# Sums of the first layer's gate and up weights moved into the first projection, and the context's gate and up products in scaled half-precision pairs

## The chip, the cores and the metric

The kernel runs on one core of one Trainium2 chip. The core has a matrix engine (PE, with its weight loads shown apart as PEld), a vector engine (DVE), a scalar engine (ACT), a general engine (POOL, also called GpSimd), and a queue engine (SP) that only issues transfers. Each of them takes its instructions in the order of its own program, and semaphores tie them together. The metric is the time of one execution in device microseconds (us); less is better. Three executions of the kernel before gave 2910.8, 2915.75 and 2916.38 us, a median of 2915.75 us.

## The reference: what is computed

The model has two layers on 1024 latent tokens and 256 context tokens of width 1024, all in float32. Cut to what matters:

```python
def swiglu(u, w_gate, w_up, w_down):
    return (jax.nn.silu(u @ w_gate) * (u @ w_up)) @ w_down

for i in range(DEPTH):                       # two layers
    ...                                      # adaLN, then a mixer, as below
    y_lat, y_ctx = mixer(...)                # layer 0: Fourier and Hyena; layer 1: neighbourhood attention
    h_lat = h_lat + g1 * y_lat
    h_lat = h_lat + g2 * swiglu(modulate(rms_norm(h_lat, norm2_g[i]), sh2, sc2), ffn_w_gate[i], ffn_w_up[i], ffn_w_down[i])
    if not last:                             # only layer 0 has a context FFN
        h_ctx = h_ctx + cg1 * y_ctx
        h_ctx = h_ctx + cg2 * swiglu(modulate(rms_norm(h_ctx, norm2_g[i]), csh2, csc2), ffn_w_gate[i], ffn_w_up[i], ffn_w_down[i])
return rms_norm(h_lat, final_g)
```

The hidden width is 2816, which the kernel cuts into 22 blocks of 128. Latent and context tokens share all weights.

## The kernel before

**Precision.** PE multiplies at full rate only in reduced formats, so every product is taken as three: an operand is split into a high part and the rest, and high·high, high·low and low·high are summed. Two kinds of pairs are in use. In the float32 kind (`split`, L285 to L289) the two parts are rounded float32 tiles ("fp32r" in the profile; the matmuls then show as f32). In the half-precision kind (`half_split`, L1215 to L1219) ACT multiplies the source by a scale and rounds it to f16 (L1218), and DVE computes the rest in one operation (L1219). The half kind needs a scale for each weight, which keeps it in the range of f16. It is found from the sums of the absolute values: `abs_sums` (L1247) has ACT read a 128x1024 tile and add up (L1251), writing the values themselves into a scratch tile `junk` of the pool T; `scale_cols` (L1311) then adds over partitions with one small matmul and takes a bound and its reciprocal on DVE (L1316 to L1318).

**Stages.** In the order of time: filters of the Hyena part; the first projection (`in_proj`, about 205 to 460 us of the profile), in half pairs, 16 blocks of 72 matmuls; Hyena and Fourier transforms; the output projection (`out_proj`, about 724 to 846 us), first for context tokens and the first 512 latent ones, then for the other 512; the context's gate and up products (851 to 983 us); the latent gate and up products of layer 0 by a Strassen-Winograd scheme with 11 pairs of blocks (983 us on); the down product; then layer 1 with attention.

**The context's gate and up products** stand at the head of `ffn` (L1519 on). For each of the 22 blocks the gate and the up weight (512 KB each) are loaded by SP into a tile of the pool S4 (20 tiles), split into float32 pairs by ACT and DVE, and multiplied with the context activations `uf`: 24 matmuls of 128x256 each. ACT applies Silu (L1529), DVE multiplies (L1530), POOL stores the result. The pair tiles come in turn from three sets of two tiles, the tags "wh"/"wl" twice and "ws" once (`pair3`), in the last two blocks from "wh"/"wl" alone (`pair1`). Between the blocks, one step of `wino_second` prepares Winograd operands of the latent activations.

**The Winograd products** (`wino_weights`, L1395 on) load four quarters of a weight, one half of them into a "ws" tile (two exist) and the other into S4. Where a weight's scale isn't known (`if key not in self.wsc`), they are summed on the spot: two passes on ACT and the chain behind. In layer 0 it is known for block pair 0 alone; for pairs 1 to 10 it is summed there.

**Sums taken ahead.** `qkv_sums` (L1253) runs beside `out_proj`, three 512 KB loads after each of its 16 output blocks: 44 loads into S4 tiles, issued by POOL, each followed by one `abs_sums` pass on ACT. The first four are gate and up of layer 0, pair 0; then come the attention's weights, then gate and up of layer 1, pairs 0 and 1.

**What sets the order.** The program text isn't the order of the engines: a planner in the framework walks through the instructions with its own estimate of their durations and gives each engine a fixed order, the earlier text first among what is ready. Work without inputs, such as a load, can so come far ahead of its place. On the chip the order stays as planned: an instruction that waits holds all behind it on its engine. Tiles of a pool are reused, so a load can also wait for the last reader of the tile.

**Beside the first projection** run `fill` generators: `filt` (the context's filters, one step per output block; their constants are loaded into "ws" tiles) and `ada` (32 reductions of adaLN weights, loaded by SP, two per block; DVE line L470, half of which write into tiles of T). T has 6 tiles and, in this stage, 4 more of the pool TK.

**After the first half of `out_proj`** (`after1`), the context activations are normalised: DVE and ACT write `uf` in float32 pairs (`norm_block`), unscaled.

Of the kernel before, what the change touches and what calls it, by code (L numbers as in the profile page):

```python
# [19 lines left out]
P = 128  # L20
# [11 lines left out]
KSTART = (0, 8, 24, 32)  # L32
PAD_C, PAD_T, SHIFT = 176, 160, 16
BOPS = ("B11", "B21", "T2", "T1", "T3", "B22", "T4")
# [167 lines left out]
class Builder:  # L202
# [176 lines left out]
    def weights16(self, src, scale, w=1024, cut=False, load=None):  # L379
        st = self.pw.tile([P, 1024], F32, tag="ws", name=self.nm("ws"))  # L380
        hi, lo = (self.pw.tile([P, 1024], F16, tag=g, name=self.nm(g)) for g in ("wh", "wl"))
        (load or self.ld)(st.rearrange("p (n k) -> p n k", n=4) if cut else st[:, :w], src)
        self.half_split(st[:, :w], scale, hi[:, :w], lo[:, :w])
        return hi, lo

# [829 lines left out]
    def half_split(self, src, scale, hi, lo):  # L1215

        nc = self.nc
        nc.scalar.activation(hi, src, AF.Copy, scale=scale)  # L1218
        nc.vector.scalar_tensor_tensor(lo, src, scale, hi, op0=MUL, op1=SUB)  # L1219

# [32 lines left out]
    def qkv_sums(self):  # L1253

        a = self.a
        self.qs = self.C(44)
        src = [a["wv"][ch, kp] for ch in range(2) for kp in range(4)]
        src += [a[n][b] for n in ("wq", "wk", "w_out2") for b in range(KB)]
        for l, i in ((0, 0), (1, 0), (1, 1)):
            src += [a[n][l, 2 * i + k] for n in ("gate", "up") for k in (0, 1)]  # L1260
        for j, k in enumerate((32, 33, 34, 35, *range(32), *range(36, 44))):
            t = self.S4()
            self.ldr(t, src[k])
            self.abs_sums([t], self.qs[:, k:k + 1])
            if j % 3 == 2:
                yield
        yield

    def first_scales(self, l):

        keys = [(l, i, m) for i in range(l + 1) for m in (0, 1)]
        n, k = len(keys), 3 * len(self.wsc)
        q = self.qs[:, 32 + 4 * l:36 + 8 * l]
        s, inv = self.scale_cols(q, self.wcol, k, n)
        for j, key in enumerate(keys):
            self.wsc[key] = (s[:, j:j + 1], inv[:, j:j + 1])
# [214 lines left out]
    def ffn(self, l, u, h, hs, second, after, keep=None, begun={}):  # L1491
# [28 lines left out]
        if u is not None:  # L1520
            for fb in range(NFB):
                wide = 3 if fb < NFB - 2 else 2
                gh, gl = self.weights(a["gate"][l, fb], wide=wide)
                uh, ul = self.weights(a["up"][l, fb], wide=wide)
                lo = self.last_lo
                ga = self.lin(gh, gl, 0, range(KB), u, (2,))[2]
                ua = self.lin(uh, ul, 0, range(KB), u, (2,))[2]
                t = self.T()
                nc.scalar.activation(t[:, :256], ga[:, :256], AF.Silu)  # L1529
                nc.vector.tensor_tensor(t[:, :256], ua[:, :256], t[:, :256], MUL)  # L1530
                self.ldr(hidc[fb // 2][:, fb % 2], t[:, :256])
# [590 lines left out]
    def run(self):  # L2122
# [98 lines left out]
        for i in range(8):  # L2221
            self.tap(f"u{i}", u.ap(0, i, 0))
        self.in_proj(u, ((filt, 1), (ada, 2)))
        drain(ada)
# [58 lines left out]
        def after1(pcs):  # L2283
            spill(h, hs0, pcs)
            if 0 in pcs:
                uf.t.update(self.new_act(pcs=(2,)).t)
                rs = self.rms(pcs)
                for b in range(KB):
                    self.norm_block({b: h.ap(0, b, 2)}, b, 2, 0, 3, uf, rs[0])
                load_h((1,))  # L2290
                self.ucol, self.usi = self.operand_scale(0, 3, (0, 1))
                self.first_scales(0)
                for _ in self.wino_first(h, 0, 3, rs[1]):
                    pass
            else:
                rest.append(self.rms((1,))[0])
# [215 lines left out]
```

## Time and profile before

| what | value |
|---|---|
| median of three executions | 2915.75 us (2910.8 to 2916.38) |
| the profiled execution's own time | 2919.95 us |
| its span from first to last instruction | 2918.2 us |
| mean granted PE clock | 0.977 |
| read from and written to memory | 455.33 MB and 135.53 MB |

The profile is of one execution, which took 4.2 us more than the median. In its rows, a matmul's duration is longer than the distance to the next, since matmuls are pipelined: the pace is read from the starts. "[2.33 <-ACT wh L287]" behind a row says that the engine was idle for 2.33 us before it and that ACT's line 287, writing the tile wh, ended that. "x2" means two instructions in a row. In a table of windows each engine's column is its busy time in us with the count of its instructions, followed by the granted PE clock, the share of time that the transfer engines were busy, and GB/s.

### The profile page before, as it was taken

The page shows a single profiled execution, that of the slowest core. Times are in us where ns is not written, and L with a number is a line of the kernel's source. Part 1 is how long each engine was busy: PE and PEld are TensorE (multiplying, and loading weights), DVE is VectorE, ACT ScalarE, POOL GpSimd, SP SyncE. Part 2 cuts the span into 40 slices and gives each one's busy share as a digit, 9 for nine tenths or more (in the row PEclk, how much of TensorE's full clock was granted, in tenths as well). Part 3 has the DMA queues.
Part 4 walks back from the last instruction along what each step waited for, and adds up shares of the span by engine and source line. Part 5 has one row for each costly group of instructions (what it writes and reads, how often), then busy time and mean ns, then how long its engine had stood idle before and what let it go on. Part 6 is the DMA issues. An engine that isn't in the chain of part 4 may idle for free. (4 is left out here: it accounts for less than half of the span.)

```text
span 2918.2 us, 46050 instructions
## 1 busy us (share of the span) xinstructions
PE 2766.6 (95%) x16163; PEld 1714.2 (59%) x16163; DVE 2094.0 (72%) x3833; ACT 1647.7 (56%) x2899; POOL 642.6 (22%) x1057
## 2 busy tenths in 40 slices
PE   6989999999989999999999999999999999999998
PEld 3766557888879644444555844676665444444554
DVE  4778867585467798877886767776676778775765
ACT  4674324454675667654555555676664477654553
POOL 1012013354220121213120012444443022112000
PEclk8989999999999999999999999999999999999999
DMA  6574434358785555566994798777775666424753
GB/s 254 187 265 161 161 122 151 111 168 286 285 344 182 207 205 197 201 213 240 327 333 161 273 337 294 179 188 172 185 198 188 236 226 231 153 93 184 242 191 113
DMA packets 325156, 615.98 MB, mean 211 GB/s; under 512 B 90934, under 2 KB 130552, under 8 KB 324922
## 3 DMA queue, kind: packets, MB, share of 16 engines
q1 hardware_dynamic: 252378, 384.38, 39.9%
q0 software_dynamic: 70240, 224.45, 21.6%
q10 hardware_dynamic: 2304, 4.20, 0.4%
q8 instruction: 127, 2.08, 0.3%
q14 instruction: 107, 0.88, 0.1%
HBM read 455.33 MB, written 135.53 MB: 202 GB/s over the span
## 5 line engine op out<-in xcount | busy, mean ns | idle before, releaser
L1449 PE MATMUL ps<-s,s 128*128 128x512 f16 x2592 | 582.2, 382 | 14.4 <-ACT tk L1454 6.8
L1449 PEld LDWEIGHTS <-s 128*128 128x128 f16 x2640 | 259.0, 98 | 332.6 <-issue 27.8
L283 PE MATMUL ps<-s,wh 128*128 128x256 f32 (+3 forms) x1752 | 398.2, 331 | 11.1 <-ACT wh L287 5.4
L1218 ACT ACTIVATE s<-s,c 128x512 f16<-128x512 f32 (+1 forms) x324 | 233.5, 754 | 141.9 <-DMA s<-d 79.9
L1219 DVE SCALAR_TENSOR_TENSOR s<-s,c,s 128x512 f16<-128x512 f32 (+1 forms) x324 | 247.4, 794 | 84.5 <-ACT s L1218 84.1
L1666 PE MATMUL ps<-s 128*128 128x512 f16 (+2 forms) x1308 | 303.4, 378 | 2.0 <-DVE s L1219 2.0
L283 PE MATMUL pq<-s,wh 128*128 128x512 f16 (+1 forms) x1000 | 280.3, 354 | 9.8 <-DMA wh<-d 5.4
L283 PE MATMUL ps<-s,wl 128*128 128x256 f32 (+3 forms) x876 | 261.6, 331 | 1.3 <-DVE wl L289 1.2
L283 PEld LDWEIGHTS <-wh 128*128 128x128 f16 x1664 | 160.9, 99 | 170.2 <-issue 20.9
L1666 PEld LDWEIGHTS <-s 128*128 128x128 f16 x1536 | 148.5, 98 | 178.9 <-issue 6.5
L274 POOL DMA_DIRECT2D d<-s x201 | 109.0, 543 | 640.5 <-DVE s L1510 178.6
L283 PE MATMUL ps<-s,s 128*128 128x65 f16 (+5 forms) x2666 | 222.3, 236 | 27.5 <-DMA s<-s 11.4
L335 ACT CAST mat<-cs 128x1024 fp32r<-128x1024 f16 (+2 forms) x120 | 111.6, 935 | 140.6 <-PE ps L283 57.3
L283 PEld LDWEIGHTS ps<-s,wh 128*128 128x128 f32 x1088 | 177.5, 192 | 18.1 <-ACT wh L287 5.7
L283 PE MATMUL ps<-s,mat 128*128 128x512 f32 x696 | 184.7, 413 | 3.3 <-DVE s L289 2.9
L1449 PE MATMUL ps<-s,wh 128*128 128x512 f16 x616 | 184.9, 379 | 1.8 <-DVE g L1463 1.4
L283 PE MATMUL pq<-s,wl 128*128 128x512 f16 (+1 forms) x500 | 174.5, 354 | 0.5 <-DMA wl<-d 0.5
L283 PEld LDWEIGHTS <-s 128*128 128x128 f16 x2400 | 114.5, 98 | 82.9 <-DMA s<-s 11.5
L283 PEld LDWEIGHTS ps<-s,mat 128*128 128x128 f32 x696 | 136.5, 199 | 37.9 <-DVE s L289 3.8
L1251 ACT ACTIVATE t<-s 128x1024 bf16<-128x1024 f32 (+1 forms) x164 | 141.9, 867 | 12.2 <-DVE c L470 8.4
L283 PEld LDWEIGHTS ps<-s,s 128*128 128x128 f32 (+1 forms) x746 | 113.6, 192 | 32.1 <-ACT s L287 7.0
L283 PEld LDWEIGHTS <-wl 128*128 128x128 f16 x832 | 82.3, 99 | 77.4 <-issue 4.5
(431 smaller groups left out, 5477.3 us busy)
## 6 DMA issues: line engine op xcount, KB each, us to landing
s<-d SPq DMA_DIRECT2D x294, 256.0 KB, 4.0
d<-s POOLq DMA_DIRECT2D x157, 256.0 KB, 3.2
s<-in_down SPq DMA_DIRECT2D x154, 256.0 KB, 5.4
s<-in_ada_w POOLq DMA_DIRECT2D x48, 512.0 KB, 4.8
g<-in_bias POOLq DMA_DIRECT2D x128, 192.0 KB, 3.6
s<-in_gate SPq DMA_DIRECT2D x46, 512.0 KB, 3.7
s<-in_up SPq DMA_DIRECT2D x46, 512.0 KB, 4.0
d<-g POOLq DMA_DIRECT2D x87, 256.0 KB, 2.9
```

The source lines that it names most:

```text
L274: self.last_ldr = self.nc.gpsimd.dma_start(out, in_).ins
L283: self.nc.tensor.matmul(o, l, r, start=st, stop=sp)
L335: self.nc.scalar.copy(m, st)
L1218: nc.scalar.activation(hi, src, AF.Copy, scale=scale)
L1219: nc.vector.scalar_tensor_tensor(lo, src, scale, hi, op0=MUL, op1=SUB)
L1251: self.nc.scalar.activation(junk[:, :t.shape[1]], t, AF.Abs, scale=2.0 ** -15, accum_out=st[:, k:k + 1])
L1449: nc.tensor.matmul(ps, x[:, sl], y, start=first and j == 0 and x is wh and y is xh, stop=j == 3 and x is wl, skip_group_check=True)
L1666: m = nc.tensor.matmul(acc[j][:, c0:c1], x[:, sl], y[:, xs], start=first and k == 0, stop=last and k == 2, skip_group_check=True)
```

## The change

1. `qkv_sums` loses its first four loads; 40 remain, and the column block `qs` shrinks from 44 to 40.
2. A new generator `gate_sums` loads the gate and up weights of all 11 block pairs of layer 0 (44 loads of 512 KB, issued by POOL, into the two "ws" tiles) and sums each on ACT. It runs beside `in_proj` as a third `fill`, three loads per output block, and is drained behind it.
3. `first_scales(0)` takes scales for all 22 weights of layer 0 from these sums, so that `wino_weights` finds each key known and does no summing in layer 0.
4. The context's gate and up products use half pairs: `weights3` splits by `half_split` with the known scale, in the same three tile sets, and in all 22 blocks. The inverse scales go into the Silu (an argument of the ACT instruction) and into the product (a `scalar_tensor_tensor` with the inverse in place of `tensor_tensor`).
5. `uf` becomes scaled half pairs: `norm_half` in place of `norm_block`, behind `load_h((1,))` and `operand_scale`. It takes four tiles of the pool S2 where it took eight.
6. A padding tile shrinks from 176 to 136 columns to make room for 44 columns of sums.

```diff
-PAD_C, PAD_T, SHIFT = 176, 160, 16
+PAD_C, PAD_T, SHIFT = 136, 160, 16
...
+    def weights3(self, src, scale):
+        self.p3 = (getattr(self, "p3", 0) + 1) % 3
+        tags = ("ws", "ws") if self.p3 == 0 else ("wh", "wl")
+        st = self.S4()
+        hi, lo = (self.pw.tile([P, 1024], F16, tag=g, name=self.nm(n)) for g, n in zip(tags, ("wh", "wl")))
+        self.ld(st, src)
+        self.half_split(st, scale, hi, lo)
+        return hi, lo
...
     def qkv_sums(self):
-        self.qs = self.C(44)
+        self.qs = self.C(40)
         src = [a["wv"][ch, kp] for ch in range(2) for kp in range(4)]
         src += [a[n][b] for n in ("wq", "wk", "w_out2") for b in range(KB)]
-        for l, i in ((0, 0), (1, 0), (1, 1)):
-            src += [a[n][l, 2 * i + k] for n in ("gate", "up") for k in (0, 1)]
-        for j, k in enumerate((32, 33, 34, 35, *range(32), *range(36, 44))):
+        src += [a[n][1, 2 * i + k] for i in (0, 1) for n in ("gate", "up") for k in (0, 1)]
+        for j, k in enumerate(range(40)):
             t = self.S4()
             self.ldr(t, src[k])
             self.abs_sums([t], self.qs[:, k:k + 1])
...
+    def gate_sums(self):
+        a = self.a
+        self.fs = self.C(4 * (NFB // 2))
+        for j in range(4 * (NFB // 2)):
+            t = self.pw.tile([P, 1024], F32, tag="ws", name=self.nm("ws"))
+            self.ldr(t, a[("gate", "up")[j // 2 % 2]][0, j // 4 * 2 + j % 2])
+            self.abs_sums([t], self.fs[:, j:j + 1])
+            yield
...
     def first_scales(self, l):
-        keys = [(l, i, m) for i in range(l + 1) for m in (0, 1)]
+        keys = [(l, i, m) for i in range(2 if l else NFB // 2) for m in (0, 1)]
         n, k = len(keys), 3 * len(self.wsc)
-        q = self.qs[:, 32 + 4 * l:36 + 8 * l]
+        q = self.qs[:, 32:40] if l else self.fs
...
             for fb in range(NFB):
-                wide = 3 if fb < NFB - 2 else 2
-                gh, gl = self.weights(a["gate"][l, fb], wide=wide)
-                uh, ul = self.weights(a["up"][l, fb], wide=wide)
+                (gs, gi), (us, ui) = (self.wsc[(l, fb // 2, m)] for m in (0, 1))
+                gh, gl = self.weights3(a["gate"][l, fb], gs)
+                uh, ul = self.weights3(a["up"][l, fb], us)
...
-                nc.scalar.activation(t[:, :256], ga[:, :256], AF.Silu)
-                nc.vector.tensor_tensor(t[:, :256], ua[:, :256], t[:, :256], MUL)
+                nc.scalar.activation(t[:, :256], ga[:, :256], AF.Silu, scale=gi)
+                nc.vector.scalar_tensor_tensor(t[:, :256], ua[:, :256], ui, t[:, :256], op0=MUL, op1=MUL)
...
-        self.in_proj(u, ((filt, 1), (ada, 2)))
+        gsum = self.gate_sums()
+        self.in_proj(u, ((filt, 1), (ada, 2), (gsum, 3)))
+        for _ in gsum:
+            pass
...
             if 0 in pcs:
-                uf.t.update(self.new_act(pcs=(2,)).t)
                 rs = self.rms(pcs)
-                for b in range(KB):
-                    self.norm_block({b: h.ap(0, b, 2)}, b, 2, 0, 3, uf, rs[0])
                 load_h((1,))
                 self.ucol, self.usi = self.operand_scale(0, 3, (0, 1))
+                for b in range(KB):
+                    if b % 2 == 0:
+                        self.new_half(uf, ((b, 2), (b + 1, 2)))
+                    self.norm_half(h.ap(0, b, 2), b, 2, uf, rs[0], self.ucol)
                 self.first_scales(0)
```

More of the change, by code (lines that the diff above doesn't have):

```diff
@@ L1218, in half_split @@
         nc.scalar.activation(hi, src, AF.Copy, scale=scale)
-        nc.vector.scalar_tensor_tensor(lo, src, scale, hi, op0=MUL, op1=SUB)
+        self.last_lo = nc.vector.scalar_tensor_tensor(lo, src, scale, hi, op0=MUL, op1=SUB).ins
     def operand_scale(self, l, m, conds):
```

## The prediction

> **What bounds the kernel now.** I read the head of the page first, then windows by stage, then in each stage that the change touches the rows of PE, of ACT and of the transfers.
>
> ```profile
> span 2918.2 us, 46050 instructions
> ...
> PE 2766.6 (95%) x16163; PEld 1714.2 (59%) x16163; DVE 2094.0 (72%) x3833; ACT 1647.7 (56%) x2899; POOL 642.6 (22%) x1057
> ```
> ```profile
> core 0: us, PE busy (x) PEld busy (x) DVE busy (x) ACT busy (x) POOL busy (x), PEclk, DMA share, GB/s
> 205.00:460.00 255.00, 246.93 (x1356) 140.65 (x1357) 198.91 (x411) 89.88 (x160) 44.06 (x51) 0.97 0.44 157
> ...
> 851.00:983.00 132.00, 127.25 (x1067) 125.03 (x1068) 93.87 (x118) 76.64 (x110) 11.91 (x22) 0.97 0.63 232
> 983.00:1290.00 307.00, 296.96 (x1373) 133.59 (x1371) 268.46 (x488) 204.39 (x389) 59.48 (x110) 0.99 0.58 207
> ```
>
> PE is the bound nearly everywhere: 95% of the span, and 97% in each of the three stages that matter (first projection, context gate and up, first part of the latent products). So the change can only win through the pace of PE's matmuls and through PE's few holes, some 8, 5 and 10 us in these stages, and the slow clock behind a hole. Work taken from ACT or DVE counts only where it stands in front of such a hole.
>
> **1. The pace of the context's matmuls.** Block by block 24 matmuls of 128x256, 44 times, so 1056. The float32 ones, and half-precision ones of the same shape in attention:
>
> ```profile
> 902.90 0.39 PE L283 MATMUL ps<-s,wh 128*128 128x256 f32 x2
> ...
> 903.24 0.39 PE L283 MATMUL ps<-s,wh 128*128 128x256 f32 x2
> ...
> 1822.11 0.38 PE L283 MATMUL pq<-s,wh 128*128 128x256 f16 x2
> ...
> 1822.44 0.38 PE L283 MATMUL pq<-s,wh 128*128 128x256 f16 x2
> ```
>
> Three start 0.34 us apart from the next three in float32, 0.33 in half precision: 0.0033 us a matmul, times 1056 is **3.5 us**. That is all that the format itself gives. Bounds 0 and 3.5.
>
> What the split costs more lies beside PE. The nearest rows:
>
> ```profile
> L289 DVE TENSOR_TENSOR wl<-s,wh 128x1024 fp32r<-128x1024 f32 x44 | 53.7, 1225 | 31.6 <-ACT wh L287 31.6
> L287 ACT CAST wh<-s 128x1024 fp32r<-128x1024 f32 x44 | 45.8, 1048 | 40.6 <-issue 26.4 <-PE ps L283 13.4 <-DMA s<-in_up 0.8
> ```
> ```profile
> L1219 DVE SCALAR_TENSOR_TENSOR wl<-ws,c,wh 128x1024 f16<-128x1024 f32 x17 | 21.8, 1282 | 7.5 <-ACT wh L1218 7.5
> L1218 ACT ACTIVATE wh<-ws,c 128x1024 f16<-128x1024 f32 x17 | 19.5, 1150 | 8.1 <-PE ps L1449 5.1 <-DVE c L1317 3.0
> ```
>
> ACT 0.10 and DVE 0.06 us more for each of 44 tiles, 4.5 and 2.5 us in all, and for the product with the inverse scale perhaps another microsecond of DVE. Over 132 us ACT has 77 and DVE 94, so both stay below PE's pace, with weights split ahead: cost 0. Without that cover it would be the 3.5 us of DVE.
>
> **2. The start of the context stage.** Here is PE's dearest hole of these stages.
>
> ```profile
> 850.00:860.00 10.00, 8.08 (x49) 7.79 (x50) 4.89 (x5) 6.54 (x10) 0.00 (x0) 0.67 1.03 421
> ```
> ```profile
> 845.44 0.40 PE L283 MATMUL ps<-s,wl 128*128 128x512 f32 x1
> ...
> 851.46 0.79 PE L283 MATMUL ps<-s,wh 128*128 128x256 f32 x2 [2.33 <-ACT wh L287]
> ...
> 853.09 0.63 PE L283 MATMUL ps<-s,wh 128*128 128x256 f32 x2
> ...
> 853.73 0.63 PE L283 MATMUL ps<-s,wh 128*128 128x256 f32 x2
> ```
> ```profile
> 816.17 1.59 POOL L274 DMA_DIRECT2D s<-in_wk  x3
> ```
> ```profile
> DMA packets 2779, 10.04 MB, mean 418 GB/s; under 512 B 333, under 2 KB 333, under 8 KB 2776
> ...
> s<-in_gate SPq DMA_DIRECT2D x7, 512.0 KB, 13.7
> ```
>
> But for a microsecond of small sums, PE has no work from 845.84 (845.44 + 0.40) to 851.46, 5.6 us, because the first context weight isn't split. Then it runs slowly: three matmuls take 0.64 us (853.09 to 853.73) instead of 0.34, for about 5 us, which loses 5 x (1 - 0.34/0.64) = 2.3 us more. The cause is in the last fence: from 836 to 860 the transfer engines are full (418 GB/s), and a weight takes 13.7 us to land. What fills them are the sums' loads: three behind each of the eight blocks of the first half of `out_proj` are 24 of the 44; then the spills of that half stand in POOL's queue, and the other 20 go out from 816 on. Without four, 16 are left behind the spills: 4 x 0.524 MB = 2.1 MB less, at 418 GB/s 5.0 us earlier. With a hole of half a microsecond the slow clock should go as well: 5.0 + 2.3 = 7.3 at best of 7.9. I take **6.5**, since SP's loads also wait for S4 tiles. Bounds 0 (another wait holds the split) and 7.9.
>
> The scaled `uf` is prepared between the halves of `out_proj`, a whole half ahead of its use. Its wait for `operand_scale` costs nothing: the reduction over partitions on POOL is planned far ahead.
>
> ```profile
> 420.85 0.38 POOL L1238 PARTITION_ALL_REDUCE c<-c  x1 [5.73 <-issue]
> ```
>
> **3. No sums in the Winograd products of layer 0.** Twenty weights, two passes each, 40 x 1.05 us of ACT gone. PE's holes there:
>
> ```profile
> PE ps L1449 <- ACT g L1454: 4.2, 3, 2.9
> PE ps L1449 <- ACT tk L1454: 4.0, 2, 2.9
> ```
> ```profile
> 987.96 2.75 PE L1449 MATMUL ps<-s,s 128*128 128x512 f16 x12 [0.67 <-ACT g L1454]
> 993.58 4.24 PE L1449 MATMUL ps<-s,s 128*128 128x512 f16 x12 [2.87 <-ACT g L1454]
> ...
> 1276.61 4.37 PE L1449 MATMUL ps<-s,s 128*128 128x512 f16 x12 [2.91 <-ACT tk L1454]
> ```
> ```profile
> 991.92 1.04 ACT L1251 ACTIVATE t<-s 128x1024 bf16<-128x1024 f32 x1
> ...
> 992.96 0.57 ACT L1454 COPY g<-ps 128x512 f32<-128x512 f32 x1
> ...
> 1274.95 1.05 ACT L1251 ACTIVATE t<-s 128x1024 bf16<-128x1024 f32 x1
> ...
> 1275.99 0.57 ACT L1454 COPY tk<-ps 128x512 f32<-128x512 f32 x1
> ```
>
> PE waits for ACT's copies out of PSUM, and right in front of both late copies stands a weight's pass. Idle behind ACT: 4.2 + 4.0 = 8.2; slow clock (4.24 - 2.75) + (4.37 - 2.75) = 3.1. Not all of it is the sums': splits stand in that queue too. One or two passes before each late copy are 2 x 1.05 a hole, 4.2, and nearly half the slow clock: **5.5**. Bounds 0 and 11.3. By the Trainium skill (TensorE: Matmul & The Clock Gate, Part 1) the clock halves only after an idle window of about 3.4 us; here 2.9 us were enough. By that rule 3.1 of the bound would not be there to win, and the term would be 4.2.
>
> **4. The end of the context stage.** Before, the last two blocks left the "ws" tiles alone; now their turn goes on, and the last pair of "ws" is freed behind block 20's up product, one block (48 x 0.11 = 5.3 us) before the stage ends.
>
> ```profile
> 967.58 0.33 SPq L268 DMA_DIRECT2D ws<-in_gate  x1
> ```
>
> The first Winograd weight was loaded 15.4 us before 983; it now comes some 10 us later, with 4 to 5 us to land and 1.15 to be split: just in time, and DVE, busy for 268 of the next 307 us, gets its work later. **-2**; bounds 0 and -5. SP's loads behind that one wait with it, but are needed later.
>
> **5. The first projection.** Here 44 loads (23.1 MB) and 44 passes of ACT come in, 46 us. On average there is room: ACT has 90 of 255 us, and 23.1 MB over 255 us add 91 to 157 GB/s, where 418 were seen. Two "ws" tiles at 4.3 us to land, half a microsecond to issue, 1.05 to sum and a microsecond of waiting turn 44 loads in 22 x 7 = 154 us, so they end inside. What they can harm is the order. At the start, 1 MB ahead of the first weights of `in_proj` is 2.5 us where transfers are full. Later, a pass can hold ACT:
>
> ```profile
> s<-in_ada_w SPq DMA_DIRECT2D x31, 512.0 KB, 4.3
> ```
> ```profile
> ACT t L1251 <- DVE c L470: 8.4, 2, 5.5
> ```
> ```profile
> 289.17 1.06 ACT L1251 ACTIVATE t<-s 128x1024 bf16<-128x1024 f32 x1 [2.97 <-DVE c L470]
> ...
> 298.37 0.59 PE L283 MATMUL ps<-s,wh 128*128 128x256 f16 x2 [3.84 <-DVE c L1316]
> ```
> ```profile
> 290.00:300.00 10.00, 5.83 (x37) 4.67 (x36) 10.00 (x21) 5.41 (x13) 2.46 (x5) 0.84 0.64 230
> 300.00:310.00 10.00, 10.00 (x51) 5.88 (x49) 10.00 (x23) 0.37 (x1) 2.91 (x4) 0.81 0.69 250
> ```
>
> A pass writes its scratch into a tile of T that an adaLN reduction on DVE (L470) still held, ACT stood still, and the weight's scale came late to PE: 3.84 us idle and about 10 x (0.16 + 0.19) = 3.5 us of clock. Queued behind a waiting pass are the next block's split and the copies out of PSUM; PE has about one block (some 15 us) of slack for them. POOL's queue now waits for "ws" tiles in front of the Fourier stores, which are read only after the stage; the context filters' constants on SP wait for a turn of "ws". I take **-6**: the 2.5 at the start and half of one more such event. Bounds 0 and -25 (the rival below).
>
> **The sum.** 3.5 + 6.5 + 5.5 - 2 - 6 = 7.5 us. Against the profiled execution's 2919.95 that is 2912.5; it was 4.2 above the median, so against 2915.75 it is **2908 us**.
>
> **Rivals.** *Slower: ACT's order in the first projection.* In 255 us some 16 passes met 8.4 us of waits for T, 0.53 each; 44 more make 23, and as 3.84 + 3.5 of those 8.4 reached PE, 20 us, with 2.5 at the start: -23 in place of -6, and 2915.75 + 9.5 = 2925. For it: DVE, which frees the tiles, is full (10.00 of 10) from 290 to 310, and two "ws" tiles leave little lead, so that a pass is soon waiting for its own load too. Against: ACT idles 165 of 255 us. It decides once the first projection is 13.5 us longer (3.5 + 6.5 + 5.5 - 2). The Trainium skill (TensorE: Matmul & The Clock Gate, table of specifications) gives ACT a strict first-in first-out queue; the trace agrees, as ACT stood 2.97 us before 289.17.
>
> *Hidden gains.* The context's own loads fill the transfers in place of the four, and ACT's relief meets no hole: 3.5 + 1 - 2 - 3, 2916. For it: the transfers stay full up to 860, behind the first weight. Against: what comes behind it cannot hold it back.
>
> *All holes close.* 3.5 + 7.9 + 11.3, without a cost: 2893. Against: the planner's order shifts with every change, and nothing in the rows makes the new one free of waits.
>
> *The change does not do what it says:* the sums might run past the first projection. That needs 11.6 us a turn instead of 7, and harms only if they last to 800; under 1 in 50.
>
> **Chances.** Forecast (2901 to 2914) 0.42; slower 0.27; hidden 0.17; all holes 0.14. The range 2896 to 2928 leaves out the far ends of two of them. A run can tell about 0.2%, 5.8 us, from none: below 2909.9 lie three quarters of the forecast and all of the last, 0.45; above 2921.6 nine tenths of the slower and a little of the rest, 0.27; between, 0.28.
>
> **What would show it.** Starts of three context matmuls 0.33 apart; a hole of under 2 us before the first of them and a granted clock near 1 behind it; no L1251 on "ws" tiles between 983 and 1290, and late copies under 1 us; a first "ws" load of the Winograd stage some 5 us before its first matmul; a first projection of 255 + 6 us. It is wrong if ACT's waits for T or for "ws" loads in the first projection reach PE for more than 13.5 us, or if the first context matmul still comes 5 us behind the last of `out_proj`.

## The result and the profile after

The changed kernel took 2925.36 us, the median of 20 runs, and the kernel before, measured beside it, 2915.88 us, also 20 runs. The ratio is 1.0032, 95% interval [1.002, 1.0043]: the change costs 0.3%, some 9 us. A second measurement gave 1.0029 [1.0011, 1.0047]. The forecast was 2908. Ratios are over the fast executions: one of sums_60 below (9989.5 us, one of eight, still counted in its median) and one of the kernel before beside it (4100.8 us, one of nineteen) are not in them.

The two profiled executions of the changed kernel took 2915.7 and 2918.1 us, the low end of its times. So the stages below show where time went, and the ratios show how much. (The two profiled executions of the kernel before took 2919.95 and 2915.97 us.)

| stage, us | before | before, again | after | after, again |
|---|---|---|---|---|
| first projection | 254.2 | 253.0 | 276.0 | 277.4 |
| Hyena, Fourier, first half of `out_proj` | 335.2 | 336.0 | 342.8 | 343.5 |
| second half of `out_proj`, context gate and up | 186.1 | 189.4 | 172.5 | 173.0 |
| Winograd products of layer 0, to the first down matmul | 400.9 | 400.9 | 389.7 | 389.8 |
| from there to the end of PE's last matmul | 1526.2 | 1525.7 | 1514.6 | 1515.6 |

Each boundary is the start of a stage's first matmul in the timeline of PE; only the first row ends with the projection's own last matmul, and the second row ends where the 128x1 matmuls of the norm start. What stands ahead of the projection (197 to 208 us) and behind the last matmul (10 to 13 us) is in no row. A stage repeats within about 1.5 us from one profile to the other, apart from 3.3 once, so the differences in the first four rows stand out from it: the projection lost 23 us and the stage behind it 7; 15 came back in the second half of `out_proj` and the context, and 11 in the Winograd stage. Where the 7 us of the second row come from is not shown. The last row differs by 11 us although the change edits nothing there. Over all the kernels below it lies between 1515 and 1529 in no order that I can explain; it is left open. So the profiles place 4 to 5 us of loss, up to the first down matmul; with the last row these two executions are not slower than those of the kernel before, and the rest of the 9 us isn't located.

The same stages of the changed kernel, as windows, and four short windows in the projection (each engine's busy time and count, then the granted PE clock, the share of the transfers and GB/s):

```profile
205.00:481.00 276.00, 251.82 (x1354) 142.59 (x1355) 189.29 (x396) 134.40 (x245) 65.24 (x93) 0.93 0.63 218
...
824.00:996.00 172.00, 168.86 (x1275) 144.01 (x1275) 129.45 (x174) 114.73 (x170) 24.62 (x46) 0.98 0.70 258
996.00:1386.00 390.00, 386.61 (x1790) 174.65 (x1791) 329.43 (x527) 211.95 (x392) 83.98 (x156) 1.00 0.61 214
220.00:230.00 10.00, 2.60 (x4) 1.29 (x5) 6.76 (x8) 2.47 (x4) 6.36 (x4) 0.62 0.22 85
230.00:240.00 10.00, 7.67 (x20) 3.23 (x19) 8.76 (x17) 5.49 (x9) 1.94 (x3) 0.53 0.52 167
350.00:360.00 10.00, 5.66 (x17) 2.24 (x18) 7.99 (x18) 5.52 (x9) 1.05 (x2) 0.66 0.75 246
380.00:390.00 10.00, 6.97 (x28) 5.02 (x29) 8.36 (x18) 7.06 (x13) 1.58 (x3) 0.52 0.50 179
```

The transfers carry 218 GB/s, less than the 248 (157 + 91) that the prediction reckoned for the old length, and are not full. PE loses its time in three places, and the granted clock of the windows with and behind them is 0.52 to 0.66. PE's rows there:

```profile
223.26 0.79 PE L283 MATMUL ps<-s,s 128*128 128x512 f32 x1 [3.29 <-ACT s L287]
...
229.42 1.65 PE L283 MATMUL ps<-s,s 128*128 128x512 f32 x3 [3.80 <-DVE s L289]
234.25 1.01 PE L283 MATMUL ps<-s,wh 128*128 128x512 f16 x2 [2.33 <-DVE c L1334]
...
354.34 1.03 PE L283 MATMUL ps<-s,wh 128*128 128x256 f16 x3 [4.46 <-ACT wh L1227]
...
383.03 1.23 PE L283 MATMUL ps<-c,tk 128*128 128x1 f32 x5 [5.03 <-ACT s L759]
```

**The first hole** comes from POOL. The line L635 (L626 before) folds the weights of the context's filter. The timeline of POOL, then the answer for that line with its instructions in POOL's queue, in the changed kernel:

```profile
208.39 0.53 POOL L274 DMA_DIRECT2D ws<-in_up  x1 [21.52 <-ACT tk L1260]
209.43 0.53 POOL L274 DMA_DIRECT2D ws<-in_up  x1 [0.51 <-ACT tk L1260]
221.31 6.36 POOL L635 TENSOR_TENSOR t<-s,s 128x512 f32<-128x512 f32 x4 [11.34 <-DMA s<-in_ada_w]
```
```profile
L635 POOLq EVENT_SEMAPHORE  x2: 43/43/43, 209.5 to 210.3; - x2
L635 POOLq MODIFY_POOL_CONFIG  x2: 37/37/37, 210.0 to 210.1; - x2
```

and the same line in the kernel before:

```profile
L626 POOL TENSOR_TENSOR t<-s,s x4: 1266/1760/2246, 208.7 to 213.3; 128x512 f32<-128x512 f32 x4
...
L626 POOLq MODIFY_POOL_CONFIG  x2: 54/54/54, 183.8 to 183.9; - x2
```

Before its first fold POOL changes its configuration, and 11.2 us pass until the fold starts (210.1 to 221.31). Before the change that happened at 183.8, under the 25 us in which the fold waited for its weights anyway. Now two loads of the sums stand in front in POOL's queue; they wait 21.52 us for a pass to free a "ws" tile, and the change of configuration comes only behind them. By then the fold's weights are there: its two waits for them (EVENT_SEMAPHORE, at 209.5 and 210.3) last 43 ns each. The profile blames a transfer ("<-DMA s<-in_ada_w"): that is the event that came last, not the cause. The Trainium skill (GPSIMD Engine Reference, 2.1 Instruction dispatch) says that the first call of a freshly loaded POOL kernel pays about 6 us for the load of its code, with no instruction in the profile for it, and counts it from this MODIFY_POOL_CONFIG. The trace agrees in kind, but the gap here is longer, 10.5 to 11.2 us in four profiles.

**The other two holes** stand behind passes that wait for their own loads. ACT's waits for the sums between 205 and 481 us (total, times, longest), and ACT's rows ahead of the two holes:

```profile
ACT t L1260 <- DMA ws<-in_gate: 28.3, 11, 6.5
ACT t L1260 <- DMA ws<-in_up: 21.1, 9, 5.0
...
ACT tk L1260 <- DMA ws<-in_up: 9.6, 3, 4.2
...
ACT t L1260 <- DVE t L680: 0.5, 1, 0.5
```
```profile
344.76 1.06 ACT L1260 ACTIVATE t<-ws 128x1024 bf16<-128x1024 f32 x1 [2.44 <-DMA ws<-in_up]
...
351.06 1.06 ACT L1260 ACTIVATE t<-ws 128x1024 bf16<-128x1024 f32 x1 [1.12 <-DMA ws<-in_gate]
...
353.15 1.13 ACT L1227 ACTIVATE wh<-s,c 128x1024 f16<-128x1024 f32 x1
```
```profile
381.36 1.06 ACT L1260 ACTIVATE t<-ws 128x1024 bf16<-128x1024 f32 x1 [5.73 <-DMA ws<-in_gate]
...
382.42 0.56 ACT L759 COPY s<-ps 128x512 f32<-128x512 f32 x1
```

The split at 353.15, for which PE stood 4.46 us, comes behind passes that stood 2.44 and 1.12 us for their loads and took a microsecond each. The copy at 382.42, for which PE stood 5.03 us, is right behind a pass that stood 5.73 us for its load. In all there are 59 us of such waits in 23 passes. The wait for a tile of T, on which the prediction's rival was priced, is 0.5 us in all.

### The profile page after: what moved, and what is told of

Same layout as the page of the kernel before. It is cut to its first block, busy times and chain, and to the rows that moved or that the text cites. A ratio compares the mean times of both kernels' runs of the same rounds, so it can differ in the third digit from the quotient of the medians.

```text
span 2913.9 us, 46029 instructions
## 1 busy us (share of the span) xinstructions
PE 2761.8 (95%) x16143; PEld 1692.6 (58%) x16143; DVE 2089.2 (72%) x3753; ACT 1650.3 (57%) x2899; POOL 660.3 (23%) x1097
## 5 line engine op out<-in xcount | busy, mean ns | idle before, releaser
L1467 PE MATMUL ps<-s,s 128*128 128x512 f16 x2064 | 464.0, 379 | 4.5 <-ACT g L1472 2.4
L283 PE MATMUL ps<-s,wh 128*128 128x256 f16 (+3 forms) x1752 | 392.6, 329 | 8.9 <-ACT wh L1227 6.2
L283 PEld LDWEIGHTS <-wh 128*128 128x128 f16 x2368 | 230.7, 99 | 186.5 <-issue 26.5
L283 PE MATMUL ps<-s,wl 128*128 128x256 f16 (+3 forms) x876 | 259.3, 329 | 1.1 <-DVE wl L1228 0.9
L1467 PE MATMUL ps<-s,wh 128*128 128x512 f16 x616 | 186.5, 382 | 4.5 <-ACT wh L1227 4.5
L283 PE MATMUL ps<-s,mat 128*128 128x512 f32 x696 | 183.8, 412 | 3.6 <-DVE s L289 3.3
L283 PEld LDWEIGHTS <-wl 128*128 128x128 f16 x1184 | 116.9, 99 | 83.8 <-issue 6.8
L1467 PE MATMUL pq<-s,s 128*128 128x512 f16 x576 | 133.3, 380 | 0.6 <-ACT tk L1472 0.4
L1227 ACT ACTIVATE s<-t,c 128x512 f16<-128x512 f32 x172 | 115.1, 711 | 27.7 <-DVE t L1446 20.9
```

Source lines behind the costliest of these rows:

```text
L283: self.nc.tensor.matmul(o, l, r, start=st, stop=sp)
L1467: nc.tensor.matmul(ps, x[:, sl], y, start=first and j == 0 and x is wh and y is xh, stop=j == 3 and x is wl, skip_group_check=True)
```

## The experiments

Ratios are against the kernel before, timed on the same chip beside it; 0.0010 of a ratio is 2.9 us. The intervals reach some 3 to 7 us to each side, so I read a kernel's projection and its third stage, the second half of `out_proj` with the context, from the profile too; these repeat better (see the first table). The kernels ran in four groups, each on one chip: the first four rows; consts_s4 to sums_part_only; pool_first, pool_first_consts, sums_s4_lag and s4_fewer; free_loads_only, s4_wino_passes and sums_60. Across groups only the ratios are compared.

| kernel | median us | ratio, 95% | projection | third stage |
|---|---|---|---|---|
| after, again | 2922.58 | 1.0029 [1.0011, 1.0047] | 277.4 | 173.0 |
| no_sums | 2902.75 | 0.9954 [0.9938, 0.997] | 251.5 | 186.3 |
| loads_only | 2916.76 | 1.0014 [0.9998, 1.0029] | 271.4 | 186.8 |
| passes_only | 2901.45 | 0.9956 [0.9943, 0.9969] | 251.1 | 186.8 |
| consts_s4 | 2915.66 | 0.9993 [0.9978, 1.0009] | 271.3 | 171.1 |
| sums_s4 | 2908.17 | 0.9970 [0.9958, 0.9981] | 255.6 | 186.5 |
| sums_hyena | 2995.57 | 1.0268 [1.0248, 1.0288] | 252.9 | 187.5 |
| sums_part_only | 2929.51 | 1.0042 [1.0027, 1.0056] | 276.6 | 176.5 |
| pool_first | 2915.05 | 0.9996 [0.9982, 1.001] | 267.7 | 171.6 |
| pool_first_consts | 2914.21 | 0.9998 [0.9982, 1.0015] | 257.8 | 188.3 |
| free_loads_only | 2901.59 | 0.9947 [0.9929, 0.9964] | 258.0 | 184.3 |
| sums_s4_lag | 2905.04 | 0.9971 [0.9957, 0.9984] | 254.2 | 186.5 |
| s4_fewer | 2896.10 | 0.9943 [0.992, 0.9965] | 255.0 | 172.2 |
| s4_wino_passes | 2913.79 | 0.9992 [0.998, 1.0005] | 255.1 | 184.3 |
| sums_60 | 2904.11 | 0.9955 [0.9937, 0.9973] | 254.9 | 173.3 |

### What the sums cost: loads and passes apart

First the changed kernel unchanged, for a second profile, and the kernel before likewise (one execution, 2915.97 us).

> The changed kernel once more, for a second profile and more times; nothing is edited. The medians so far are 2925.4 us for it and 2915.9 for the kernel before, but the profile at hand is of an execution of 2915.7. If those 10 us are in the first projection, its last matmul comes near 491 us of the profile instead of 481; if they are spread over the kernel, the first projection again ends near 481 and each later stage ends a few us later. Time: 2925, between 2916 and 2934.

> The kernel before once more, for a second profile: the one at hand is of an execution of 2920.0 us, 4 over the median. If its slower parts are the same ones as in the changed kernel, nothing changes; expected is a first projection of 253 to 255 us, a hole of some 5 us before the first context matmul, and a time of 2908 to 2920 us.

Both profiles repeated the first ones; the projection of the changed kernel ended at 481 us in both. The second profile, too, is of an execution at the low end (2918.1 us), so where the other 7 us of the median go is not seen.

```diff
-        for j in range(4 * (NFB // 2)):
-            t = self.pw.tile([P, 1024], F32, tag="ws", name=self.nm("ws"))
-            self.ldr(t, a[("gate", "up")[j // 2 % 2]][0, j // 4 * 2 + j % 2])
-            self.abs_sums([t], self.fs[:, j:j + 1])
-            yield
+        self.nc.vector.memset(self.fs, 7.8e-4)
+        yield
```

> The changed kernel without the 44 loads and the 44 passes of ACT: the column block is filled with a constant of the usual size, all else is as in the change. It gives the whole price of the sums in the first projection. Theory (the sums cost the 19.4 us by which the first projection was longer, the rest of the change gains 10): 2906 us, first projection back at 256 us. Rival (most of the 19.4 us is given back by the stages behind, which wait for transfers anyway, and the loss lies elsewhere in the change, in the context or Winograd stage): 2918 or more, though the first projection is short again.

> The 44 loads into the two tiles stay, the 44 passes are left out, the sums are a constant. Theory (the passes stand in ACT's order and wait for their own loads): the loads alone cost about 4 us, the 2.5 us at the start and a little for the w3 loads there, so 2910 us. Rival (the transfers are what is dear: 23.1 MB more, and full transfer engines delay the weights of the projection): 2922 to 2926 us, the first projection still some 19 us longer.

> The 44 passes of ACT stay, but read a resident tile, half precision, 128x1024; the 44 loads are left out and the sums are a constant. Theory (it is the wait for the own load that holds ACT): the passes never wait, 46 us go into ACT's idle time, cost 0 to 4 us: 2906 to 2910 us. Rival (the passes as such are dear, by 46 us of ACT or by the tiles of T that they write): 2920 to 2926 us.

The diff is no_sums. In loads_only only the line with `abs_sums` gives way to the constant; in passes_only the tile and the load go, and the pass is `self.abs_sums([self.resident], ...)`, a part of `u`. Without sums the ratio is 0.9954 against 1.0029 on the same chip: the sums cost 0.75%, 22 us, and the rest of the change gains 13. The passes as such cost nothing (0.9956, projection 251.1). The loads alone cost 0.6%, 17 us, and the projection is 20 us longer than in no_sums: the theory missed, the rival was nearer. But most of that is the order of a queue and not GB/s. SP's, PE's and DVE's timelines in loads_only:

```profile
407.19 2.90 SPq L268 DMA_DIRECT2D cs<-in_vf_l  x2
410.15 0.42 SPq L268 DMA_DIRECT2D s<-in_w_in  x1
```
```profile
427.19 1.25 PE L283 MATMUL pq<-s,wh 128*128 128x512 f16 x3 [6.69 <-DVE s L783]
436.69 0.16 PE L283 MATMUL ps<-st,c 128*128 128x2 bf16 x1 [6.75 <-DVE st L1318]
```
```profile
417.11 1.23 DVE L479 CUSTOM_DVE_ANT_0 t<-s,s 128x1024 bf16<-128x1024 f32 x1 [16.30 <-DMA s<-in_ada_w]
```
```profile
SPq L268 <- DMA ws<-in_up: 32.9, 5, 19.2
```
```profile
435.40 0.38 POOL L1247 PARTITION_ALL_REDUCE c<-c  x1 [5.73 <-issue]
```

The fourth is the table of SP's waits, with one of 19.2 us, and the last is POOL's timeline. The constants "cs" live in "ws" tiles; the load at 407.19 waited for the sums' loads to leave one, and the projection's own weight (410.15) and the adaLN weights stood behind it on SP; DVE stood 16.30 us for the latter. PE paid 13.4 us. The second half of that has POOL's all-reduce in it (last row): its 5.73 us of "issue" were there before too, and the prediction put them at nothing since they came far ahead of need; behind the late adaLN weights they come too late for PE.

### Which queue, which tiles

```diff
-        st = self.pw.tile([P, w], F16, tag="ws", name=self.nm("cs"))
+        st = self.S4(F16, w) if getattr(self, "own", False) else self.pw.tile(
+            [P, w], F16, tag="ws", name=self.nm("cs"))
```

> The change, with the constants of the context's filters loaded into S4 tiles instead of ws tiles while the sums run; the sums keep the two ws tiles to themselves. Theory (the sums share the two ws tiles with constants that SP loads; SP waits for its turn, 19.2 us at one place in the run with the loads alone, and the projection's weights and adaLN loads stand behind it): the 14.0 us that the loads cost alone shrink to the 4 us at the start; with the 5.8 us of the passes some 2912 us. Rival (23.1 MB more are dear as such, whatever the tiles): 2919 to 2925 us.

The flag `own` is set while `in_proj` and what is drained behind it are written out. It falls between the two: 0.9993, 10 us better than the change; the projection 271.3 instead of 277. POOL's hole is still there (fold at 216.1), so the theory named one cause of several. Of the other two holes the later one is gone; at the place of the earlier one PE still waits 2.3 and 4.4 us.

```diff
-            self.ldr(t, a[("gate", "up")[j // 2 % 2]][0, j // 4 * 2 + j % 2])
+            with self.follow(self.last_fold):
+                self.ldr(t, a[("gate", "up")[j // 2 % 2]][0, j // 4 * 2 + j % 2])
```

> The change, with the sums' loads held on POOL's queue behind the four fold instructions of the context's filter (L635), nothing else edited. In the changed kernel two of these loads wait on POOL for their turn of a ws tile until 209.4 us; only behind them POOL changes its configuration, and 11.3 us later the first fold starts at 221.3, where it started at 208.7 before. Theory (this change of configuration lost its cover and PE fell 14 us behind there): first fold near 209 us, PE's waits for L287 and L289 between 220 and 235 us gone, and as later stages gave back half of what the projection lost, 2908 to 2916 us. Rival (the fold waits for its own loads or for full transfers): fold still at 218 or later, 2919 us or more.

`last_fold` is the last L635 instruction. As expected: 0.9996, 10 us better. POOL's timeline:

```profile
202.63 6.38 POOL L635 TENSOR_TENSOR t<-s,s 128x512 f32<-128x512 f32 x4 [25.57 <-DMA s<-in_w]
208.96 1.28 POOL L274 DMA_DIRECT2D ws<-in_gate  x2
```

The fold now starts when its own weights land, 5.0 us behind the projection's first matmul (197.6) instead of 16.3 (205.05 to 221.31), and the projection is 9 us shorter. This, with the 43 ns in the changed kernel, shows the cause of the first hole: neither its own loads nor the transfers held the fold.

Then both edits in one kernel (pool_first_consts), and the same without the line `self.abs_sums([t], self.fs[:, j:j + 1])` (free_loads_only).

> Both: the sums' loads behind the folds, and the constants of the context's filters in S4 tiles, so that SP doesn't wait for a ws tile. The passes still have only two ws tiles. Theory (POOL's change of configuration, SP's wait and the passes' wait for their own loads are three separate parts): near the loads in S4, 2905 to 2912 us, with the passes' waits of some 60 us on ACT still there and one or two of them reaching PE. Rival (one cause in two dresses): no better than the better of the two alone.

> As pool_first_consts (loads behind POOL's folds, constants in S4, the sums' loads alone on the two ws tiles), but without the 44 passes; the sums are a constant. pool_first_consts was no better than pool_first, 2915 us, where 2905 to 2912 was expected. Theory (what is left there is the passes, which with two tiles wait for their own loads in front of splits and copies): 2902 to 2907 us. Rival (23.1 MB through POOL's queue and the transfers cost the rest): 2911 us or more.

Both edits together shorten the projection by 19 us, to 257.8, yet the time is no better than with one (0.9998). The table says why: the third stage went from 172 to 188, and gave the gain back. free_loads_only (the two edits, no passes) has about the time that the theory gave, but the same projection, 258.0. That equal length doesn't show the passes to be free, for the holes differ. With the passes PE waits 3.81 and 4.62 us for splits. Without them it waits 6.41 us at another place, where a load that waits for its turn of "ws" holds POOL's own work (L1015):

```profile
264.80 1.03 PE L283 MATMUL pq<-s,wh 128*128 128x512 f16 x2 [6.41 <-DVE s L764]
```
```profile
259.33 0.53 POOL L274 DMA_DIRECT2D ws<-in_gate  x1 [4.03 <-DMA ws<-in_up]
259.88 1.28 POOL L1015 TENSOR_TENSOR tk<-s,s 128x511 f32<-128x511 f32 x1
```

So even in these two kernels POOL's queue isn't free. The 15 us between their ratios are none in the projection and none in the Winograd stage, but 3 to 6 us each in the other stages (4 of them ahead of the projection, where nothing was edited); the two ran on different chips, and this pair leaves open where they come from.

```diff
-            t = self.pw.tile([P, 1024], F32, tag="ws", name=self.nm("ws"))
+            t = self.S4()
```

> The change, with the sums' 44 loads in tiles of S4 instead of ws: the constants have the ws tiles alone, and a load can run ahead of its pass by more than two. Theory (the shared pair of ws tiles is the cause, by SP's waits and by passes without lead): 2903 to 2909 us, near the 2902.8 of no sums at all. Rival (transfers as such): 2917 or more. A third way: S4 has no tiles to spare, the projection's weights then wait for theirs, 2915 or more, and PE's holes show waits for w_in.

```diff
-            self.abs_sums([t], self.fs[:, j:j + 1])
+            if j >= 3:
+                self.abs_sums([t[j - 3]], self.fs[:, j - 3:j - 2])
```

> The loads in S4 tiles as in sums_s4, and each pass stands three loads behind its own load in the text. In sums_s4 PE still waited 2.7 and 4.9 us for a copy behind a pass. Theory (the passes' waits for their own loads are the last 4 to 5 us of the price): 2902 to 2906 us and no wait of ACT for these loads over 2 us. Rival (four loads in flight take S4 tiles from the projection's weights, or the transfers themselves are the rest): 2908 us or more.

Out of the "ws" tiles, the sums leave SP's constants alone, and their loads need no pass to have ended, so POOL comes to its fold in time: 0.9970, faster than the changed kernel and the one before it, the projection 255.6. With the pass three loads behind its load (sums_s4_lag) the projection is 254.2, as before the change, and the time the same (0.9971): it gave 1.4 us where I expected up to 5.

```diff
-        self.in_proj(u, ((filt, 1), (ada, 2), (gsum, 3)))
+        self.in_proj(u, ((filt, 1), (ada, 2)))
...
         def every(g, n):
             for i, _ in enumerate(g):
+                next(gsum, None)
```

> The change, with the same loads into ws tiles and the same passes one stage later, one after each step of the Hyena transforms, where the transfers were 0.4 busy between 500 and 580 us before. Theory (two ws tiles shared with SP's constants are the cause): these stages load their constants through ws too, so it is no better there: 2918 to 2930 us. Rival (the full transfers at the start of the projection and its weights are the cause): 2905 to 2910 us.

Direction right, size far off: 1.0268. One table of PE's waits in this kernel, 455 to 1075 us:

```profile
PE ps L283 <- ACT mat L335: 34.6, 29, 4.0
PE ps L283 <- ACT wh L287: 23.8, 4, 14.6
```

The first line is the cost of sharing: 29 waits for a constant that came late through "ws". In the kernel before, from 455 to 980 us, it is 1.7 us in 2 waits.

### The start of the context stage

```diff
-        for j, k in enumerate(range(40)):
+        self.nc.vector.memset(self.qs[:, 24:40], 7.8e-4)
+        for j, k in enumerate(range(24)):
```

> The loads in S4 tiles as in sums_s4, and beside out_proj the last 16 of its 40 sums are left out (w_out2, and gate and up of layer 1), with constants in their place: 8.4 MB less where transfers are full. In sums_s4 and in no_sums PE waits 7 to 8 us for a w_out weight at 848 to 853 us, one block before the place of the hole of the kernel before. Theory (the hole went from the context's first weight to the last w_out weight, since the transfers are still full of sums): that wait falls under 2 us and the slow matmuls behind it go, some 10 us: 2896 to 2900 us. Rival (SP's loads wait for S4 tiles, or the spills fill the transfers): the wait stays over 5 us, 2904 us or more.

```diff
+        late = [a["w_out2"][b] for b in range(KB)]
+        late += [a[n][1, 2 * i + k] for i in (0, 1) for n in ("gate", "up") for k in (0, 1)]
+        todo += [(x, self.qs[:, 24 + j:25 + j]) for j, x in enumerate(late)]
...
-        self.in_proj(u, ((filt, 1), (ada, 2), (gsum, 3)))
+        self.in_proj(u, ((filt, 1), (ada, 2), (gsum, 4)))
```

> A version that computes everything: the 44 sums in S4 tiles with the pass three loads behind, as in sums_s4_lag, and the last 16 sums of out_proj (w_out2, and gate and up of layer 1) moved into the first projection too, four loads per block instead of three. Theory (the hole at 848 to 855 us is the price of these 16 loads in out_proj, and the projection has room for 31.5 MB where no queue is held up): the hole goes as in s4_fewer, the projection stays at 254 to 258 us, 2895 to 2901 us. Rival (60 loads fill the projection's transfers, or S4 tiles run short): the projection 265 us or longer, 2905 us or more.

Where the projection ends early, the third stage has its hole again, only one block ahead of its old place. PE in no_sums, and the window 840 to 850 us of no_sums and then of sums_60:

```profile
841.20 0.40 PE L283 MATMUL ps<-s,wl 128*128 128x512 f32 x1
848.55 0.80 PE L283 MATMUL ps<-s,wh 128*128 128x512 f32 x1 [6.95 <-ACT wh L287]
```
```profile
840.00:850.00 10.00, 3.05 (x12) 1.77 (x10) 2.91 (x4) 6.29 (x9) 0.54 (x1) 0.81 1.02 416
```
```profile
840.00:850.00 10.00, 10.00 (x45) 8.20 (x44) 5.83 (x7) 2.51 (x4) 1.08 (x2) 1.00 0.69 242
```

With the last 16 sums left out of `out_proj` (s4_fewer) the stage is 172.2 instead of 186.5 and the time 0.9943: the transfers, full at 416 GB/s, were what the w_out weight waited for. sums_60 computes these 16 too, but in the projection (w_out2, and gate and up of layer 1 behind the 44, four loads a block): 242 GB/s at that place, no hole, 173.3, and a projection of 254.9 with 60 loads in it. It has the lowest ratio of the kernels that compute everything, 0.9955 [0.9937, 0.9973], 13 us faster than before, though its interval overlaps that of sums_s4; the 2895 to 2901 us that I expected would have needed 2 us more.

### The half pairs and the Winograd passes

```diff
-                gh, gl = self.weights3(a["gate"][l, fb], gs)
-                uh, ul = self.weights3(a["up"][l, fb], us)
+                wide = 3 if fb < NFB - 2 else 2
+                gh, gl = self.weights(a["gate"][l, fb], wide=wide)
+                uh, ul = self.weights(a["up"][l, fb], wide=wide)
```

> The moved sums alone: the context's gate and up products stay in float32 pairs with unscaled activations, everything else is as in the change. It tells what the half pairs give. Theory (0.0033 us a matmul, 3.5 us, less 2 at the end of the stage, where the ws tiles are freed later): 2922.6 + 1.5 = 2924 us, between 2922 and 2926. Rival (the half pairs give more, since they relieve the start of the context stage): 2928 or more. Rival (they cost): under 2921.

The Silu, the product and `norm_block` are as before too. It is at 1.0042 where the change is at 1.0032 and 1.0029: the half pairs give about 3 to 4 us, inside the measurement's doubt. (By its median, 2929.5, it would lie where the rival stood; the ratio, taken beside the kernel before, is the fairer figure.)

```diff
         if key not in self.wsc:
             self.wsc[key] = self.weight_scale(st)
+        elif l == 0 and i:
+            s = self.pt.tile([P, 16], F32, tag="st", name=self.nm("st"))
+            self.abs_sums(st, s)
```

> As sums_s4, with the 40 passes of ACT over layer 0's Winograd weights done again into a column that nobody reads. Theory (the passes held up ACT's copies out of PSUM there, term of 5.5 us, bounds 0 and 11.3): 4 to 11 us more than sums_s4, the Winograd stage 395 to 401 us to the first down matmul instead of 391. Rival (ACT's passes met no hole, and the gain of that stage has another source): within 2 us of sums_s4.

This kernel is sums_s4 with these lines added. It is at 0.9992 against 0.9970 for sums_s4: 6.4 us, and the Winograd stage is 396.8 instead of 391.0. The late copies are back, with passes ahead of them on ACT. PE's waits from 983 to 1380 us in this kernel and then in sums_s4:

```profile
PE ps L1470 <- ACT g L1475: 7.7, 5, 4.2
```
```profile
PE ps L1467 <- ACT g L1472: 2.3, 2, 1.2
```

## Why the prediction was wrong

**The step that failed is term 5, the first projection: put at -6, measured at about -22** (no_sums against the change; 23 us in the projection's own length, and the stage behind it 7 longer). Its sum of bandwidth was right: 218 GB/s, full transfers only up to 220 us (329 GB/s at most in any 20 us behind), and the sums end inside the stage, at 472. Its count of harm, "the 2.5 at the start and half of one more such event", was not. It looked at ACT's queue and priced the two other queues at nothing. Of POOL it said that only the Fourier stores stand behind the loads; it passed over the four folds and the change of configuration in front of them, 9 to 10 us (pool_first). Of SP it named the constants' turn of "ws" and gave it no price; that is 5 to 6 us of the projection by consts_s4, and 13.4 us of waiting in loads_only. The two don't simply add up: together their removal takes 19 us from the projection.

**The rival "slower" had the price and the sign, 2925, and only part of the cause.** It scaled waits for tiles of T from 8.4 us to 23; they are 0.5 us. What it mentioned beside, that "a pass is soon waiting for its own load" with two "ws" tiles, is in the rows (59 us, twice reaching PE). And passes_only shows that passes without loads cost nothing, so ACT's room was as large as the prediction said. That the rival's 2925 is the measured time is therefore luck.

**Terms 1 to 4, put at 13.5 together, are 13 by no_sums, but not piece by piece.** In that kernel's profile the third stage, where terms 1, 2 and 4 should give 8, is 186.3 us against 186.1 and 189.4 before, and the Winograd stage gives 11 in place of 5.5; that the sums agree is luck.

- Term 1, the pace: put 3.5. Three context matmuls start 0.33 us apart, and sums_part_only gives 3 to 4 us, less term 4.

```profile
991.41 0.27 PE L283 MATMUL ps<-s,wl 128*128 128x256 f16 x1
991.52 0.38 PE L283 MATMUL ps<-s,wh 128*128 128x256 f16 x2
991.74 0.27 PE L283 MATMUL ps<-s,wl 128*128 128x256 f16 x1
```

- Term 2, the hole at the context's start: put 6.5. Its cause, loads of sums in full transfers, is right (s4_fewer, sums_60). Its size is not: four sums fewer don't close the hole, they leave it at the w_out weight one block earlier (6.95 us in no_sums, third stage 186.3, as before the change). In the change as it is, where PE arrives 30 us later, the hole is gone and the stage is 14 to 16 us shorter. That the later arrival is the reason was not tested by itself. For it: of the kernels with all 44 loads in the projection and 40 in `out_proj`, those whose third stage begins 611 us or more behind the projection's first matmul have no such hole, and those that begin at 607 or less have it. With the Winograd stage's 11 it brings the 30 us lost by 824 us down to 4 or 5 at the first down matmul, counted from the start of the projection.
- Term 3, the Winograd products: put 5.5. The passes alone are 6.4 us. The whole stage gained 11 (400.9 to 389.7). The rest is untested; the chain of small sums behind each pass is gone too, and may be it.
- Term 4, the end of the context stage: put -2. The first "ws" load went out at 989.97, and PE stood 1.06 us before the first Winograd matmul at 996.34, with 0.55 behind it.

```profile
989.97 0.33 SPq L268 DMA_DIRECT2D ws<-in_gate  x1
```
```profile
996.34 1.04 PE L1467 MATMUL ps<-s,wh 128*128 128x512 f16 x4 [1.06 <-ACT wh L1227]
...
997.93 0.39 PE L1467 MATMUL ps<-s,s 128*128 128x512 f16 x1 [0.55 <-ACT s L1227]
```

Of the signs that the prediction named, the pace of 0.33, the closed hole, the first "ws" load some 6 us ahead and the end of the passes on the Winograd weights came, and the late copies are 1.3 us at most where under 1 was named. The projection of 255 + 6 us did not come: it is 276.

The range, 2896 to 2928, held the result; the likeliest case did not, since its largest unknown was costed from the one queue that the trace of before happened to show waiting.

## What to carry to other kernels

When loads are added to an in-order queue, list all that stands behind them there, on every queue that shares their tiles, and ask of each instruction when it would have been ready: the room of the engine and of the transfers says nothing on it. Give added work tiles of its own, or it makes other queues wait for its turn. And compare stages, not totals: here the third stage was shorter by half of the loss where it started late, and gave back a real gain where it started early, until the full transfers behind both were relieved (sums_60).

## What was not expected of the hardware

POOL's change of configuration ahead of the folds takes 10.5 to 11.2 us from MODIFY_POOL_CONFIG to the first fold wherever nothing else covers it: 11.2 and 10.5 in the changed kernel's two profiles, 10.5 in consts_s4, 10.7 in sums_part_only. In loads_only it is 9.4 at most, for there the fold waited for its weights up to 210.3 and started at 210.4:

```profile
L635 POOLq MODIFY_POOL_CONFIG  x2: 57/57/57, 201.0 to 201.0; - x2
L635 POOLq EVENT_SEMAPHORE  x2: 43/366/689, 209.6 to 211.6; - x2
```

In the kernels where it came 20 us or more ahead of the folds it cost nothing. The profile shows no busy instruction in that gap. In consts_s4 it is called "issue", in the changed kernel a transfer; the answer for the line in consts_s4:

```profile
L635 POOL TENSOR_TENSOR t<-s,s x4: 1251/1490/2243, 216.1 to 220.2; 128x512 f32<-128x512 f32 x4
...
L635 POOLq MODIFY_POOL_CONFIG  x2: 37/37/37, 205.6 to 205.6; - x2
...
  issue: 10.6, 1
```
